# Grouped-query attention on one core: a new instruction plan, v's casts tied to VectorE passes, and reordered first loads

## The chip, the cores and the metric

The kernel runs on one core of a Trainium2 chip. A core has several engines with an instruction queue each: TensorE (matrix products, PE in the profile, with its weight loads shown apart as PEld), VectorE (DVE), ScalarE (ACT), GpSimd (POOL) and SyncE (SP, which here only issues transfers). The metric is the device time of one execution in microseconds. The profile's span, from the first to the last instruction of the program, is somewhat shorter than that time.

## The reference, cut to what matters

```python
# q: (8 batches, 8 heads, 1024, 64); k, v: (8 batches, 2 heads, 1024, 64), float32
for g in range(2):                                  # four q heads share one k and one v
    scores = (1 / 8) * matmul(q[:, 4*g:4*g+4], k[:, g:g+1].transpose(0, 1, 3, 2))
    attn = exp(scores - max(scores))
    attn = attn / (sum(attn) + 1e-8)
    output[:, 4*g:4*g+4] = matmul(attn, v[:, g:g+1])
```

There are 64 jobs (one for each batch and q head). A job has 1024 x 1024 scores. The kernel cuts them into 8 "pairs", each a tile of 128 partitions x 1024 scores in PSUM, the accumulators of TensorE. There are thus 512 pairs, and each must get its exponential. The scores are small, and no maximum is subtracted.

## The kernel before

The exponentials are shared between two engines. Most pairs go to ScalarE, which does one activation for each. The others go to VectorE, which builds the exponential from bits: one pass over the scores in PSUM (`dpass`, tile `yt`), and then, for two pairs at a time, three steps on 16-bit tiles in SBUF: `zh` and `two` (bit masks) and `mul`. For the last two jobs a fourth step, `add`, joins the two parts; for the others TensorE multiplies both parts (`et`, `zt`) with v and so adds them in its accumulator.

```python
# one event of the plan after the other; the engines' queues get their instructions in this order
elif kind == "score":                               # TensorE: one pair, two matmuls
    where_s[(j, c)] = new_slot(x)                   # one of three PSUM slots
    ...
elif kind == "act":                                 # ScalarE: one pair
    exps.append(nc.scalar.activation(out=p, in_=where_s[(j, c)], func=AF.Exp, scale=scale))
    if len(exps) % 12 == 0 and len(exps) > 16: ...  # waits for an exp 15 back
elif kind == "dpass":                               # VectorE: one pair
    nc.vector.tensor_scalar(out=yt[ch][:, i, :, :], in0=where_s[c],
                            scalar1=EXP_A, scalar2=EXP_B, op0=ALU.mult, op1=ALU.add)
elif kind == "zh": ...                              # zt = (yt & 0x7F) | 0x3F00
elif kind == "two": ...                             # et = yt & 0x7F80
elif kind == "mul": ...                             # zt = yt * zt
elif kind == "pv": ...                              # TensorE: products with v into ops (65 columns: 64 and the sum)
elif kind == "rec": ...                             # VectorE: reciprocal of 7 sums
elif kind == "norm": ...                            # VectorE: seven 64-column results times their reciprocals
```

The order of the queues comes from a `Plan` that runs on the host while the kernel is built. It steps through time with a duration for each instruction (`M_ACT` for an exp, `M_FIX + 1024 * M_D1` for a dpass, and so on) and takes at each moment the first choice that its rules allow. Up to two of a job's eight pairs go to VectorE.

v reaches SBUF as float32, and GpSimd casts it into the matmul operand `va`, one tile for each batch and v head, sixteen in all. The plan puts the cast at a fixed time before its first use:

```python
def place_v(b, g):
    return nc.gpsimd.tensor_copy(out=va[:, b * G + g, :, :, 0:D], in_=vs.pop((b, g))...)
...
ev.append((pvs[j] - 16000, "lv", None, (b, g), None))            # load of v
ev.append((max(pvs[j] - 8000, M_START), "pl", None, (b, g), None))   # the cast
```

The start of the kernel loads k, q and v of the first job, casts k and q and turns them with the identity matrix on TensorE:

```python
nc.sync.dma_start(out=f32["k"], in_=rows(k[0, 0], True))
nc.scalar.dma_start(out=f32["q"], in_=rows(q[0, 0], True))
load_v(0, 0)
...
nc.vector.tensor_copy(out=b16["k"], in_=f32["k"])
nc.scalar.activation(out=b16["q"], in_=f32["q"], func=AF.Copy)
# 4 + 4 transposes of k and q, 8 of k with its halves swapped
nc.vector.tensor_copy(out=k0[:, 0, 0:128], in_=turned["k"][:, 0:128])
nc.scalar.activation(out=qt[0][:, 0, :], in_=turned["q"], func=AF.Copy)
nc.vector.tensor_copy(out=k0[:, 0, 128:HS], in_=turned["k"][:, 128:HS])
nc.vector.tensor_copy(out=k0[:, 1, :], in_=ops[0])
```

At the end the last job's result is normalised in two halves on VectorE, each with its own reciprocal, and stored by two transfers.

Of the kernel before, what the change touches and what calls it, by code (L numbers as in the profile page):

```python
# [10 lines left out]
M_START = 5450  # L11
M_SWAP = 1200
M_Q1 = 3500
M_QSTEP = 2700
M_WARM = 7000
M_FILL = 12000
# [4 lines left out]
M_SWITCH = 92  # L21
M_MM = 33.5
M_PVTAIL = 180
M_ACT = 905
M_ATAIL = 135
M_FIX = 76
M_DTAIL = 83
# [4 lines left out]
M_REC = 115  # L32
M_GAP = 60
M_RUNWAY = 1500
M_BACK = 2500
M_WAIT = 200
STEP = 10
INF = float("inf")
PB = 7
NPIECE = 8  # L40
GRAIN = 3
MXD = 2
TAIL = 2
STEPS = (("zh", M_D4), ("two", M_D4), ("mul", M_D2), ("add", M_D2))


class Plan:


    def __init__(self, nj, npt, nct, nyt):  # L50
        self.nj, self.npt, self.nct, self.nyt = nj, npt, nct, nyt
        self.ev = []
        self.spare = None
        self.mms = [8] * nj

        self.last = (nj - 1) * NPIECE
        self.groups = [(i, min(i + PB, self.last)) for i in range(0, self.last, PB)]
        self.groups += [(self.last, self.last + 4), (self.last + 4, self.last + 8)]
        self.group_of = [g for g, (lo, hi) in enumerate(self.groups) for _ in range(lo, hi)]
        self.run()  # L60

    def run(self):
        nj, ev = self.nj, self.ev
        todo = [list(range(8)) for _ in range(nj)]
        dcount = [0] * nj
        qready = [M_START] + [M_START + M_Q1 + M_QSTEP * j for j in range(nj - 1)]
        slot_free = [M_START, M_START, M_START + M_SWAP - 600]
        aq, dq = [], []
        p_ready = [[INF] * 8 for _ in range(nj)]
        tP = tA = M_START  # L70
        tD = M_START + M_SWAP
        mode = None
        steps = list(range(8))
        dend, dlast = 0, None
        open_chain, chains, nch = None, [], 0
        norms = []
        out_free = [M_START, M_START]
        pc, done = 0, 0
        last, groups, group_of = self.last, self.groups, self.group_of
        used_p = used_c = 0  # L80
        a_of = [0] * nj
        ch_left = {}
        a = 0

        def steps_of(j):
            return STEPS if j >= nj - TAIL else STEPS[:3]

        def pick_d():
            for j in range(a, min(nj, a + 3)):
                if todo[j] and dcount[j] < MXD and qready[j] <= tP:  # L90
                    return j
            return None

        while pc < last or steps or norms:
            t = min(tP, tA, tD)
            while a < nj and not todo[a]:
                a += 1
            if tA == t:
                if aq and aq[0][0] <= t:
                    _, s, j, c = aq.pop(0)  # L100
                    ev.append((t, "act", s, j, c))
                    tA = t + M_ACT
                    slot_free[s] = p_ready[j][c] = tA + M_ATAIL + M_SEE
                else:
                    tA = t + STEP
                continue
            if tD == t:
                end = None
                if dq and dq[0][0] <= t:
                    _, s, j, c = dq.pop(0)  # L110
                    if open_chain and open_chain["steps"] != steps_of(j):
                        chains.append(open_chain)
                        open_chain = None
                    if open_chain is None:
                        open_chain = dict(id=nch, pairs=[], at=0, steps=steps_of(j))
                        ch_left[nch] = set()
                        nch += 1
                        used_c += 1
                    ch = open_chain
                    ch["pairs"].append((j, c))  # L120
                    ch_left[ch["id"]].add(j)
                    ev.append((t, "dpass", s, (ch["id"], len(ch["pairs"]) - 1), (j, c)))
                    end = t + M_FIX + 1024 * M_D1
                    slot_free[s] = end + M_DTAIL + M_SEE
                    dlast = (ch["id"], 0)
                    if len(ch["pairs"]) == 2:
                        chains.append(ch)
                        open_chain = None
                elif norms and norms[0][0] <= t and norms[0][1] == "rec":
                    _, _, lo, hi = norms[0]  # L130
                    ev.append((t, "rec", (lo, hi), None, None))
                    end = t + M_REC
                    dlast = lo
                    norms[0] = (end, "norm", lo, hi)
                else:
                    best = None
                    if norms and norms[0][0] <= t:
                        late = dlast == norms[0][2]
                        best = (late, 5 if late else 0, None)
                    for ch in chains:  # L140

                        late = dlast == (ch["id"], ch["at"]) and ch["at"] in (0, 3)
                        key = (late, 3 - ch["at"], ch)
                        if best is None or key[:2] < best[:2]:
                            best = key
                    if best:
                        at = max(t, dend + M_DEP) if best[0] else t
                        ch = best[2]
                        if ch is None:
                            _, _, lo, hi = norms.pop(0)  # L150
                            ev.append((t, "norm", (lo, hi), None, None))
                            end = at + M_FIX + 64 * (hi - lo) * M_D1
                            out_free[group_of[lo] % 2] = end + M_DTAIL + M_SEE
                            dlast = None
                        else:
                            n = len(ch["pairs"])
                            kind, rate = ch["steps"][ch["at"]]
                            ev.append((t, kind, None, ch["id"], n))
                            end = at + M_FIX + 1024 * n * rate
                            ch["at"] += 1  # L160
                            dlast = (ch["id"], ch["at"])
                            if ch["at"] == len(ch["steps"]):
                                chains.remove(ch)
                                for j, c in ch["pairs"]:
                                    p_ready[j][c] = end + M_DTAIL + M_SEE
                if end:
                    tD, dend = end, end + M_DTAIL
                else:
                    tD = t + STEP
                continue  # L170

            cold = 2 if t < M_WARM else 1
            free = [s for s in range(3) if slot_free[s] <= t]
            runway = tA - t + M_ACT * len(aq)
            slack = runway - cold * M_PAIR - M_PTAIL - (M_SWITCH if mode != "s" else 0)
            can_a = a < nj and len(aq) < 2 and qready[a] <= t and used_p < self.npt
            dj = None
            if not dq and len(chains) < self.nyt and (open_chain or used_c < self.nct):
                back = max(tD - t, 0)
                for ch in chains:  # L180
                    n = len(ch["pairs"])
                    back += sum(M_FIX + 1024 * n * r for _, r in ch["steps"][ch["at"] :])
                if back < M_BACK:
                    dj = pick_d()
            kind = None
            if free:
                if dj is not None:
                    if not can_a:
                        kind = "D"
                    elif len(free) > 1 or slack <= M_GAP or mode == "s":  # L190
                        kind = "D" if slack > M_PAIR else "A"
                elif can_a:
                    full = len(free) > 1 or mode == "s"
                    if slack <= M_GAP or (full and runway < M_RUNWAY):
                        kind = "A"
            if kind:
                if mode != "s":
                    tP += M_SWITCH
                    mode = "s"
                s = free[0]  # L200
                j = a if kind == "A" else dj
                c = todo[j].pop(0)
                ev.append((tP, "score", s, j, c))
# [6 lines left out]
                else:  # L210
                    dcount[j] += 1
                    if j < nj - TAIL:
                        self.mms[j] += 1
# [463 lines left out]
```

The softmax here doesn't subtract the row's maximum and nothing guards it: scores larger than these inputs give would overflow.

## Time and profile before

| what | value |
|---|---|
| device time, median of 3 runs | 366.85 us (366.73 to 367.86) |
| span of the profiled execution | 364.9 us |
| ScalarE busy | 355.1 us, 97% of the span |
| VectorE busy | 351.6 us, 96% |
| TensorE busy, matmuls | 346.3 us, 95% |
| GpSimd busy | 51.3 us, 14% |
| transfers | 44.81 MB, mean 123 GB/s |

Busy time of an engine is the time in which at least one of its instructions is under way. Neighbouring instructions of one engine overlap a little, so the mean duration of a group is longer than the distance from one start to the next. For TensorE's matmuls the overlap is large, and its busy share says little. In a row of the groups, "x384" is the count, then come the busy time of the group and the mean duration of one, and after the bar the idle time before them and what ended it.

### The profile page before, as it was taken

The page shows a single profiled execution, that of the slowest core. Times are in us where ns is not written, and L with a number is a line of the kernel's source. Part 1 is how long each engine was busy: PE and PEld are TensorE (multiplying, and loading weights), DVE is VectorE, ACT ScalarE, POOL GpSimd, SP SyncE. Part 2 cuts the span into 40 slices and gives each one's busy share as a digit, 9 for nine tenths or more (in the row PEclk, how much of TensorE's full clock was granted, in tenths as well). Part 3 has the DMA queues.
Part 4 walks back from the last instruction along what each step waited for, and adds up shares of the span by engine and source line. Part 5 has one row for each costly group of instructions (what it writes and reads, how often), then busy time and mean ns, then how long its engine had stood idle before and what let it go on. Part 6 is the DMA issues. An engine that isn't in the chain of part 4 may idle for free.

```text
span 364.9 us, 13795 instructions
## 1 busy us (share of the span) xinstructions
PE 346.3 (95%) x6155; PEld 220.5 (60%) x6155; DVE 351.6 (96%) x476; ACT 355.1 (97%) x387; POOL 51.3 (14%) x100
## 2 busy tenths in 40 slices
PE   7899999999999999999999999999999999999995
PEld 3466666656666665666656666655666656666664
DVE  3999999999999999999999999999999999999993
ACT  4999999999999999999999999999999999999994
POOL 3112021021211112021111112102111111211000
PEclk9999999999999999999999999999999999999999
DMA  6546768659657566856558576567685648953223
GB/s 158 94 97 120 128 121 130 156 107 159 119 89 160 120 146 99 164 111 138 132 102 156 108 141 137 125 150 107 110 164 108 145 79 157 145 122 91 69 59 88
DMA packets 89164, 44.81 MB, mean 123 GB/s; under 512 B 45488, under 2 KB 87345, under 8 KB 87857
## 3 DMA queue, kind: packets, MB, share of 16 engines
q1 hardware_dynamic: 86192, 33.31, 39.6%
q0 software_dynamic: 2496, 10.23, 21.3%
q8 instruction: 48, 0.79, 0.9%
q10 hardware_dynamic: 416, 0.39, 0.4%
q14 instruction: 12, 0.09, 0.1%
HBM read 25.17 MB, written 27.00 MB: 143 GB/s over the span
## 4 chain that ended last, share of the span: by engine, by line
ACT 56%; DVE 37%; PE 4%; DMA 1%; issue 1%
ACT pt L532 56%; DVE yt L543 16%; DVE zt L566 8%; DVE zt L550 5%; DVE ost L633 4%; DVE et L557 4%; PE sp L522 2%; DMA k<-in_k_dram 1%; DVE rec L630 1%; PE ops L584 1%; PE sp L605 1%; PE sp L438 0%; PE ops L428 0%; ACT qt L451 0%; DVE k L433 0%
## 5 line engine op out<-in xcount | busy, mean ns | idle before, releaser
L532 ACT ACTIVATE pt<-sp 128x1024 bf16<-128x1024 f32 x384 | 352.6, 1099 | 1.0 <-PE sp L522 0.7
L522 PE MATMUL sp<-qt,kt 64*128 64x512 bf16 x1024 | 173.4, 385 | 12.2 <-ACT pt L532 6.6
L584 PE MATMUL ops<-va,pt 128*128 128x65 bf16 x3024 | 184.6, 194 | 0.0
L584 PEld LDWEIGHTS <-pt 128*128 128x128 bf16 x3024 | 135.9, 97 | 43.2 <-issue 43.2
L543 DVE TENSOR_SCALAR yt<-sp 128x1024 uint16<-128x1024 f32 x128 | 155.8, 1217 | 2.3 <-PE sp L522 2.1
L584 PE MATMUL ops<-va,zt 128*128 128x65 bf16 x1008 | 124.5, 194 | 0.0
L584 PE MATMUL ops<-va,et 128*128 128x65 bf16 x992 | 120.3, 194 | 0.0
L584 PEld LDWEIGHTS <-et 128*128 128x128 bf16 x992 | 80.3, 98 | 26.0 <-issue 26.0
L584 PEld LDWEIGHTS <-zt 128*128 128x128 bf16 x1008 | 83.2, 97 | 6.9 <-issue 6.9
L522 PEld LDWEIGHTS <-kt 64*128 64x128 bf16 x1024 | 47.5, 93 | 57.6 <-issue 36.7
L566 DVE TENSOR_TENSOR zt<-yt,zt 128x2048 bf16<-128x2048 bf16 x64 | 78.0, 1220 | 0.0
L359 POOL DMA_DIRECT2D qd<-in_q_dram x63 | 32.7, 519 | 214.6 <-PE sp L522 208.5
L550 DVE TENSOR_SCALAR zt<-yt 128x2048 uint16<-128x2048 uint16 x64 | 46.4, 724 | 0.1
L633 DVE TENSOR_TENSOR ost<-ops,rec 128x448 f32<-128x448 f32 x72 | 44.2, 614 | 0.0
L557 DVE TENSOR_SCALAR et<-yt 128x2048 uint16<-128x2048 uint16 x64 | 43.2, 676 | 0.0
L367 POOL DMA_DIRECT2D kd<-in_k_dram x15 | 7.3, 488 | 64.5 <-PE sp L522 59.7
L630 DVE RECIPROCAL rec<-ops 128x7 f32<-128x7 f32 x72 | 14.1, 196 | 1.4 <-PE ops L584 1.3
L384 POOL CAST va<-vs 128x512 bf16<-128x512 f32 x16 | 10.9, 679 | 0.1
L428 PE MATMUL ops<-warm 128*128 128x128 bf16 (+1 forms) x27 | 4.8, 332 | 1.2 <-DVE warm L351 1.2
L428 PEld LDWEIGHTS <-warm 128*128 128x128 bf16 x27 | 2.2, 117 | 4.0 <-issue 2.9
L433 DVE CAST k<-k 128x512 bf16<-128x512 f32 x1 | 0.4, 427 | 2.8 <-DMA k<-in_k_dram 2.8
L434 ACT ACTIVATE q<-q 128x512 bf16<-128x512 f32 x1 | 0.6, 631 | 1.9 <-DMA q<-in_q_dram 1.9
(26 smaller groups left out, 16.4 us busy)
## 6 DMA issues: line engine op xcount, KB each, us to landing
out_dram<-ost SPq DMA_DIRECT2D x63, 256.0 KB, 2.9
qd<-in_q_dram POOLq DMA_DIRECT2D x63, 128.0 KB, 3.3
vs<-in_v_dram SPq DMA_DIRECT2D x16, 256.0 KB, 3.6
kd<-in_k_dram POOLq DMA_DIRECT2D x15, 128.0 KB, 2.9
kt<-kt SPq DMA_DIRECT2D x30, 64.0 KB, 2.8
qt<-qd SPq DMA_TRANSPOSE x63, 3.9
q<-in_q_dram ACTq DMA_DIRECT2D x1, 256.0 KB, 3.6
k<-in_k_dram SPq DMA_DIRECT2D x1, 256.0 KB, 3.7
```

The lines of the kernel that those rows point to most:

```text
L359: return nc.gpsimd.dma_start(out=t.rearrange("(a x) d -> a (x d)", x=4), in_=q[b, h].rearrange("(a x) d -> a (x d)", x=8),)
L367: return nc.gpsimd.dma_start(out=t.rearrange("(a x) d -> a (x d)", x=4), in_=k[b, g].rearrange("(a x) d -> a (x d)", x=8),)
L384: return nc.gpsimd.tensor_copy(out=va[:, b * G + g, :, :, 0:D], in_=vs.pop((b, g)).rearrange("p c (two d) -> p c two d", two=2),)
L522: now = nc.tensor.matmul(sps[x][:, half, :], lhsT=t[lo : lo + D, c // NH, ci % NH * 128 : (ci % NH + 1) * 128], rhs=qt[j][lo : lo + D, 0, ...
L532: exps.append(nc.scalar.activation(out=p, in_=where_s[(j, c)], func=AF.Exp, scale=scale))
L543: nc.vector.tensor_scalar(out=yt[ch][:, i, :, :], in0=where_s[c], scalar1=EXP_A, scalar2=EXP_B, op0=ALU.mult, op1=ALU.add,)
L550: nc.vector.tensor_scalar(out=zt[j][:, 0:c], in0=yt[j][:, 0:c], scalar1=0x7F, scalar2=0x3F00, op0=ALU.bitwise_and, op1=ALU.bitwise_or,)
L557: ins = nc.vector.tensor_scalar(out=et[j][:, 0:c], in0=yt[j][:, 0:c], scalar1=0x7F80, scalar2=None, op0=ALU.bitwise_and,)
L566: nc.vector.tensor_tensor(out=z, in0=yt[j].bitcast(BF16)[:, 0:c], in1=z, op=ALU.mult)
L584: nc.tensor.matmul(ops[plan.group_of[x] % 2][:, lo : lo + D + 1], lhsT=p[:, qs * 128 : (qs + 1) * 128], rhs=va[:, b * G + h // HPG, ci % N ...
L630: nc.vector.reciprocal(out=rec[:, 0:n], in_=o[:, :, D])
L633: nc.vector.tensor_tensor(out=ost[:, r : r + n, :], in0=o[:, :, 0:D], in1=rec[:, 0:n].unsqueeze(2).to_broadcast([128, n, D]), op=ALU.mult,)
```

## The change

The change has four parts.

1. **The plan.** Its durations are set anew: an exp from 905 to 917 ns, the fixed part of a VectorE instruction from 76 to 66 ns, a product with v from 33.5 to 31.2 ns, and others. Where TensorE has several things that it could do, the plan now tries each on a copy of its state, runs on for 7 us and adds up the idle time of ScalarE (weight 1.0) and of VectorE (weight 0.4); the choice with the least is taken. Buffers grow to fit (`pt` from 32 to 34, the chain's tiles from 7 to 8 and from 3 to 4), while k's and v's shrink (from 5 to 4, from 3 to 2). Jobs 1 and 33 may give VectorE three pairs.
2. **The casts of v.** A cast now becomes an event (`gplace`) just ahead of a VectorE pass over PSUM, and waits for the VectorE instruction in front of that pass, so that it begins when the pass begins.
3. **The first loads.** k comes in two pieces, the first v load waits until half of q is cast, the casts and the copies of k and q are shared out between VectorE and ScalarE, and the eight swapped transposes of k come behind the first score.
4. **The end.** The last job has one reciprocal over 8 sums; VectorE normalises one half and ScalarE the other with four small activations.

There is also code for doing part of `mul` on GpSimd; the constant `GC = 0` leaves it out of the program.

Counted in the order of instructions of the two kernels: exps on ScalarE go from 384 to 382, `dpass` from 128 to 130, `zh`, `two` and `mul` from 64 to 65 each, products with v from 5088 to 5104.

```diff
-M_ACT = 905
+M_ACT = 917
-M_FIX = 76
+M_FIX = 66
-M_MM = 33.5
+M_MM = 31.2
+HORIZON = 7000
+W_A = 1.0
+W_D = 0.4
+MORE = 32
+GC = 0
...
+            if s.nxt[j] < 8 and s.dcount[j] < MXD + (j % MORE == 1) and self.qready[j] <= s.tP:
...
+            kind, others = self.choices(s)
+            if others and HORIZON:
+                best = self.cost(s.copy(), kind, t + HORIZON)
+                for x in others:
+                    c = self.cost(s.copy(), x, t + HORIZON)
+                    if c < best - 1:
+                        best, kind = c, x
...
-    NPT = 32
-    NCT = 7
-    NYT = 3
+    NPT = 34
+    NCT = 8
+    NYT = 4
...
-    nc.sync.dma_start(out=f32["k"], in_=rows(k[0, 0], True))
+    for c, n in ((0, 1), (1, NH - 1)):
+        nc.sync.dma_start(out=f32["k"][:, c : c + n], in_=rows(k[0, 0], True)[:, c : c + n])
     nc.scalar.dma_start(out=f32["q"], in_=rows(q[0, 0], True))
-    load_v(0, 0)
...
-    nc.vector.tensor_copy(out=b16["k"], in_=f32["k"])
-    nc.scalar.activation(out=b16["q"], in_=f32["q"], func=AF.Copy)
+    nc.vector.tensor_copy(out=b16["k"][:, 0:1], in_=f32["k"][:, 0:1])
+    ins = nc.scalar.activation(out=b16["q"][:, 0:2], in_=f32["q"][:, 0:2], func=AF.Copy)
+    nc.vector.tensor_copy(out=b16["q"][:, 2:NH], in_=f32["q"][:, 2:NH])
+    nc.scalar.activation(out=b16["k"][:, 1:NH], in_=f32["k"][:, 1:NH], func=AF.Copy)
+    tc.add_manual_dep(load_v(0, 0).ins, ins.ins.name, Sync, reason="loads in time, not sooner")
...
+        elif kind in ("gmul", "gplace"):
+            if kind == "gplace":
+                gps = place_v(*divmod(j, G))
...
+            tc.add_manual_dep(gps.ins, vec.ins.name, Sync, reason="VectorE needs the port before")
...
-            if len(exps) % 12 == 0 and len(exps) > 16:
+            if len(exps) % (NPT - 6) == 0:
...
+                if lo >= plan.last:
+                    for i in range(4):
+                        nc.scalar.activation(
+                            out=ost[:, r + 4 + i, :], in_=o2[:, 1, i, 0:D],
+                            func=AF.Copy, scale=rec[:, 4 + i : 5 + i],
+                        )
```

## The prediction, made before the result was known

> **What bounds the kernel now.** I read the groups of the page first. Columns: line, engine, operation, tiles and shapes, count; after the first bar busy time in us and mean ns of one; after the second the idle time before them and what ended it.
>
> ```profile
> L532 ACT ACTIVATE pt<-sp 128x1024 bf16<-128x1024 f32 x384 | 352.6, 1099 | 1.0 <-PE sp L522 0.7
> L522 PE MATMUL sp<-qt,kt 64*128 64x512 bf16 x1024 | 173.4, 385 | 12.2 <-ACT pt L532 6.6
> L543 DVE TENSOR_SCALAR yt<-sp 128x1024 uint16<-128x1024 f32 x128 | 155.8, 1217 | 2.3 <-PE sp L522 2.1
> L566 DVE TENSOR_TENSOR zt<-yt,zt 128x2048 bf16<-128x2048 bf16 x64 | 78.0, 1220 | 0.0
> L550 DVE TENSOR_SCALAR zt<-yt 128x2048 uint16<-128x2048 uint16 x64 | 46.4, 724 | 0.1
> ```
>
> The exps keep ScalarE busy for 352.6 of 364.9 us with 1.0 us of idle time among them, and VectorE is also hardly ever idle. TensorE's scores wait 12.2 us, 6.6 of them for ScalarE to give a PSUM slot back: TensorE is ahead. So two engines are full at once, and the page alone does not say which one has room. The chain that ended last, taken piece by piece (start, length, what), tells more.
>
> ```profile
> 0.74 3.75 DMA k<-in_k_dram
> 9.41 19.00 ACT pt L532 x21
> 138.44 11.22 ACT pt L532 x12
> 349.28 9.18 ACT pt L532 x10
> ```
>
> 21 exps in 19.00 us are 0.905 us each; the piece at 138.44 shows 0.935. All in all ScalarE starts its first exp at 7.36 and ends its last at about 360.28, so 352.9 / 384 = 0.919 each. Compared with 0.905 that is 384 x 0.014 = 5.4 us that an exp waited for a score that came late, in waits too short to be shown as idle time. For VectorE I read the timeline of single instructions (start, length) at two casts of v, and GpSimd's beside it.
>
> ```profile
> 182.13 1.82 DVE L566 TENSOR_TENSOR zt<-yt,zt 128x2048 bf16<-128x2048 bf16 x1
> 183.87 0.19 DVE L630 RECIPROCAL rec<-ops 128x7 f32<-128x7 f32 x1
> ...
> 203.68 1.22 DVE L543 TENSOR_SCALAR yt<-sp 128x1024 uint16<-128x1024 f32 x1
> 204.81 0.61 DVE L633 TENSOR_TENSOR ost<-ops,rec 128x448 f32<-128x448 f32 x1
> 205.34 0.68 DVE L550 TENSOR_SCALAR zt<-yt 128x2048 uint16<-128x2048 uint16 x1
> 205.94 1.22 DVE L543 TENSOR_SCALAR yt<-sp 128x1024 uint16<-128x1024 f32 x1
> ```
>
> ```profile
> 182.23 0.63 POOL L384 CAST va<-vs 128x512 bf16<-128x512 f32 x1
> ...
> 204.26 0.63 POOL L384 CAST va<-vs 128x512 bf16<-128x512 f32 x1
> ```
>
> Distances between starts are the real cost: 1.13 us for a dpass, 0.53 for a norm, 0.60 for a mask step; read so along the timeline, the others are 1.13 for a mul, 0.61 for `zh` and 0.12 for a reciprocal. The mul at 182.13 stands beside a cast and takes 183.87 - 182.13 = 1.74, so 0.61 us are lost. The cast at 204.26 stands beside a dpass and a norm, and nothing is lost. I went through all sixteen: nine met a mask step or a mul and cost 0.24 to 0.80 us, 4.4 us together.
>
> **What the Trainium skill says.** "SBUF — State Buffer", section "Who interferes with whom": VectorE shares a port pair with GpSimd; an instruction in a two-port mode, and one with two SBUF inputs against a GpSimd reader, takes it for its whole length and the other blocks, while a VectorE instruction with at most one SBUF input outside those modes does not contend. The two casts above agree: the PSUM pass and the norm (one SBUF input) are untouched, the mul is held. "VectorE: DVE Perf Modes", section "The perf-mode tier table", gives 693 ns for a 16-bit `tensor_scalar` of 2048 and 1224 ns for a `tensor_tensor`; the trace has 0.68 and 1.22 us where nothing is beside them. "ScalarE: Activation LUTs", section "What ACT_TABLE_LOAD costs", puts an activation at 186 ns + 0.833 ns per column, 93 ns more for each pointer operand, and an overlap of about 93 ns back to back: 946 ns for an exp by that, where the trace shows 905, so the measurement is used.
>
> **The change part by part.**
>
> *Work moved to VectorE.* Two exps leave ScalarE: 2 x 0.905 = 1.8 us less. VectorE gets 2 x 1.13 + 0.61 + 0.60 + 1.13 = 4.6 us more. TensorE gets 16 products of 0.031 us (ten stand in 0.47 us of the timeline, less the length of one), 0.5 us, for which it has room.
>
> *Casts.* The sixteen casts stay, fifteen of them begin with a PSUM pass (1.13 us), and a cast takes 0.63. If GpSimd's queue is free at that moment, the 4.4 us go. So on VectorE the casts pay for the two added pairs nearly exactly: +4.6 - 4.4 = +0.2 us.
>
> *First loads.* Before, k lands at 4.49, then cast, eight transposes, copy of q (ends 6.68), score, exp at 7.36. After, q needs a half-width cast (0.4), four transposes (0.5), a copy of 320 columns (0.45) and the score, with k's other pieces beside it; without v's 256 KB in the way q may land 0.2 us sooner. I estimate the first exp at 6.5, 0.9 sooner. But VectorE's first dpass (7.79 before) stands in its queue behind the copy of the swapped k, which now waits for transposes that follow the first score: 6.4 + 0.65 + 0.7 = 7.8, no gain.
>
> *Plan.* What the look-ahead is worth cannot be counted from the source. The order of instructions shows that TensorE's pattern hardly changes: 272 runs of scores between products, 270 before. At best it removes ScalarE's 5.4 us of late scores.
>
> *End.* Before, two normalisations in a row end 1.18 us after the last sums (360.80 to 361.98). After, four small activations with a pointer operand: by the skill's figures 186 + 93 + 53 - 93 = about 240 ns each, an estimate, 1.0 us, after a 0.2 us reciprocal. No gain, at most 0.2.
>
> ```profile
> 358.49 0.21 DVE L630 RECIPROCAL rec<-ops 128x7 f32<-128x7 f32 x1 [1.33 <-PE ops L584]
> 360.80 0.18 DVE L630 RECIPROCAL rec<-sp 128x4 f32<-128x4 f32 x1 [1.45 <-PE sp L605]
> 361.56 0.42 DVE L633 TENSOR_TENSOR ost<-sp,rec 128x256 f32<-128x256 f32 x1
> ```
>
> **The sum, for each engine.** ScalarE: 6.5 + 382 x 0.919 (late scores as before) = 357.6, or 6.5 + 382 x 0.905 = 352.2 with none. From its last exp to the end of the span it was 364.9 - 360.3 = 4.6 us. Span 356.8 to 362.2. VectorE: up to the last dpass there stood 127 dpasses, 64 muls and adds, 63 each of the mask steps, 69 reciprocals and 69 norms: 336.9 us by the distances above. It began at 7.79 and reached the last dpass at 351.14, so 6.4 us were lost: 4.4 to casts, 0.9 between the first two dpasses, 1.1 elsewhere. After: 129, 65, 64, 64, 70, 69 make 341.6. 7.8 + 341.6 + 0.9 + 1.1 = 351.4, later than before by 0.3. Behind it stand 6.9 us of work and waits for the last products; in the lines above these are 1.33 + 1.45 = 2.8 us because ScalarE ended last. With ScalarE ahead I take half, 1.5. VectorE ends at 359.8, and the last store ends the span 2.9 us after it, as before (361.98 to 364.9): 362.7. Device time lay 366.85 - 364.9 = 2.0 above the span: 364.7. The look-ahead also counts VectorE's idle time, and I give it 0.4 us of the 1.1. **So VectorE becomes the bound, and I predict 364.3 us**, 0.7% less than before.
>
> **Rivals.**
> 1. *ScalarE stays the bound with its late scores.* For it: the number of runs of scores is the same, and three PSUM slots still feed both engines. It makes 362.2 + 2.0 = 364.2, nearly the same time, but VectorE would then wait at the end.
> 2. *The look-ahead works fully and VectorE gives way.* ScalarE's 356.8 would make 358.8. Against it: VectorE's 341.6 us to the last dpass are counted work, and no order of scores shortens them. Only a shorter start and end could, so 361 is about the floor.
> 3. *Casts still collide.* GpSimd's queue keeps its order, and q's and k's conversions (0.49 us each, waiting for scores) stand in it. If a cast starts 0.5 us late, it runs into the next mask step. With all 4.4 us back: 368 to 369.
> 4. *The plan fits less well.* It now takes 917 ns for an exp that needs 905, so it may issue scores later than ScalarE wants them. Another 3 to 5 us of late scores: 367 to 369.
>
> **Range and chances.** 364.3 is where the first two sums meet. The low end, 361.0, is rival 2 at its floor; the high end, 367.8, a half of rival 3 or 4. Over 2% faster means below 359.5, which VectorE's counted work all but excludes: 0.03. Over 2% slower means above 374.2, more than rivals 3 and 4 bring together: 0.04. That leaves 0.93 within 2%.
>
> **What would show it right or wrong.** In the profile after: casts that begin just behind the start of a dpass, and no mul or mask step above 1.3 us (step *casts*); first exp at 6.3 to 6.7 and first dpass at 7.6 to 8.0 (*first loads*); ScalarE's exps at 0.919 or longer on average with VectorE never waiting (VectorE the bound), or at 0.905 to 0.91 with VectorE's last dpass before 350 (I undercounted what the look-ahead gains); the chain's share of VectorE well above the 37% of before. A plan that leaves TensorE waiting less, and the exps longer apart, would make the prediction too low; a dpass that starts well before 7.6, or work of VectorE that I count as fixed but that shrinks, would make it too high.

## The result, and the profile after

The changed kernel takes 364.33 us at the median, the kernel before 367.37 us in the same session: a ratio of 0.9923, 95% interval 0.990 to 0.9946. It is faster by 0.8%, about 2.8 us. The predicted time was 364.3 us. Three of the six executions of the kernel before in that session took 367.86 to 368.00 us; in the four later sessions, with 113 executions, its medians are 366.63 to 366.87 us, and against those the gain is 2.3 to 2.5 us.

The chain that ended last (share of the span by engine), before the change and then after it:

```profile
ACT 56%; DVE 37%; PE 4%; DMA 1%; issue 1%
```

```profile
ACT 94%; PE 4%; issue 1%; DVE 0%
```

The groups that answer to those of before, in the same columns:

```profile
L747 ACT ACTIVATE pt<-sp 128x1024 bf16<-128x1024 f32 x382 | 350.7, 1067 | 2.0 <-PE sp L735 2.0
L735 PE MATMUL sp<-qt,kt 64*128 64x512 bf16 x1024 | 174.2, 383 | 8.9 <-ACT pt L747 4.9
L758 DVE TENSOR_SCALAR yt<-sp 128x1024 uint16<-128x1024 f32 x130 | 158.4, 1218 | 1.3 <-PE sp L735 1.1
L781 DVE TENSOR_TENSOR zt<-yt,zt 128x2048 bf16<-128x2048 bf16 x65 | 78.4, 1207 | 0.0
L765 DVE TENSOR_SCALAR zt<-yt 128x2048 uint16<-128x2048 uint16 x65 | 44.1, 679 | 0.2
```

Two things are to be seen. The chain lies on ScalarE for 94% of the span, where 37% were VectorE's before. And the mask step `zh` has come down from 724 to 679 ns on average, the mul from 1220 to 1207: nothing holds them any more. The timeline at a cast, GpSimd's first and then VectorE's, shows why:

```profile
128.93 0.62 POOL L552 CAST va<-vs 128x512 bf16<-128x512 f32 x1 [1.55 <-DVE et L772]
```

```profile
128.93 1.23 DVE L758 TENSOR_SCALAR yt<-sp 128x1024 uint16<-128x1024 f32 x1
130.07 0.61 DVE L855 TENSOR_TENSOR ost<-ops,rec 128x448 f32<-128x448 f32 x1
130.60 1.22 DVE L781 TENSOR_TENSOR zt<-yt,zt 128x2048 bf16<-128x2048 bf16 x1
```

The cast starts with the dpass, is done after 0.62 us and leaves it its 1.14 us (128.93 to 130.07). All sixteen casts lie within a dpass (the first begins 0.37 us behind its start, the others within 0.18 us of it), and none stands beside a mask step or a mul. VectorE has room at the end: its last reciprocal waits 2.42 us for TensorE's last products, which wait for ScalarE's last exps.

```profile
358.70 0.21 DVE L852 RECIPROCAL rec<-sp 128x8 f32<-128x8 f32 x1 [2.42 <-PE sp L820]
```

The profiled execution took 365.4 us, 1.1 more than the median, because TensorE's granted clock fell to a half for 3.4 us in it; that stretch is set apart below. The two profiles add up as follows, all from starts and ends in the timelines (0.903 and 0.904 us are the commonest distances of two exps):

| part of the span, us | before | after |
|---|---|---|
| up to the first exp | 7.36 | 6.33 |
| 383 or 381 distances of exps at 0.904 | 346.23 | 344.42 |
| what the distances are longer than that (late scores) | 5.47 | 6.28, of which 1.48 at the low clock |
| the last exp | 1.21 | 1.15 |
| from its end to the issue of the last store | 1.74 | 2.23 |
| from there to the end of the span | 2.85 | 3.21 |
| span | 364.87 | 363.62 |

So in these two profiles the start gives 1.0 us and the two exps 1.8; late scores fall by 0.7 outside the low clock, 0.25 of it in the first 12 us; the end takes back 0.5 and more. The 1.0 us of the start is a figure of two single executions: in the eleven traces of kernels with the new start the first exp begins between 6.12 and 6.78 us, most often near 6.56.

### The profile page after: what moved, and what is told of

It reads as the page before. It is cut to its first block, busy times and chain, and to the rows that moved or that the text cites. A ratio compares the mean times of both kernels' runs of the same rounds, so it can differ in the third digit from the quotient of the medians.

```text
span 363.6 us, 13853 instructions
## 1 busy us (share of the span) xinstructions
PE 348.0 (96%) x6179; PEld 222.5 (61%) x6179; DVE 350.6 (96%) x481; ACT 354.3 (97%) x390; POOL 50.2 (14%) x100
## 4 chain that ended last, share of the span: by engine, by line
ACT 94%; PE 4%; issue 1%; DVE 0%
ACT pt L747 94%; PE ops L799 1%; PE ops L600 1%; PE sp L735 1%; PE sp L820 1%; ACT ost L863 0%; ACT qt L624 0%; DVE qt L626 0%; DVE warm L519 0%; PE sp L614 0%
## 5 line engine op out<-in xcount | busy, mean ns | idle before, releaser
L747 ACT ACTIVATE pt<-sp 128x1024 bf16<-128x1024 f32 x382 | 350.7, 1067 | 2.0 <-PE sp L735 2.0
L799 PE MATMUL ops<-va,pt 128*128 128x65 bf16 x3008 | 182.7, 194 | 0.0
L799 PEld LDWEIGHTS <-pt 128*128 128x128 bf16 x3008 | 140.4, 98 | 34.2 <-issue 34.2
L758 DVE TENSOR_SCALAR yt<-sp 128x1024 uint16<-128x1024 f32 x130 | 158.4, 1218 | 1.3 <-PE sp L735 1.1
L799 PE MATMUL ops<-va,zt 128*128 128x65 bf16 x1024 | 136.9, 195 | 0.0
L799 PE MATMUL ops<-va,et 128*128 128x65 bf16 x1008 | 133.9, 195 | 0.0
L799 PEld LDWEIGHTS <-et 128*128 128x128 bf16 x1008 | 86.1, 98 | 30.6 <-issue 30.0
L799 PEld LDWEIGHTS <-zt 128*128 128x128 bf16 x1024 | 88.8, 98 | 7.6 <-issue 7.6
L781 DVE TENSOR_TENSOR zt<-yt,zt 128x2048 bf16<-128x2048 bf16 x65 | 78.4, 1207 | 0.0
L765 DVE TENSOR_SCALAR zt<-yt 128x2048 uint16<-128x2048 uint16 x65 | 44.1, 679 | 0.2
L820 PE MATMUL sp<-va,pt 128*128 128x65 bf16 x48 | 1.9, 194 | 0.5 <-ACT pt L747 0.5
```

Source lines behind the costliest of these rows:

```text
L758: vec = nc.vector.tensor_scalar(out=yt[ch][:, i, :, :], in0=where_s[c], scalar1=EXP_A, scalar2=EXP_B, op0=ALU.mult, op1=ALU.add,)
L765: vec = nc.vector.tensor_scalar(out=zt[j][:, 0:c], in0=yt[j][:, 0:c], scalar1=0x7F, scalar2=0x3F00, op0=ALU.bitwise_and, op1=ALU.bitwise_or,)
L781: vec = nc.vector.tensor_tensor(out=z, in0=flat(yt[j])[:, 0:c, 0 : cols[0]], in1=z, op=ALU.mult)
L799: nc.tensor.matmul(ops[plan.group_of[x] % 2][:, lo : lo + D + 1], lhsT=p[:, qs * 128 : (qs + 1) * 128], rhs=va[:, b * G + h // HPG, ci % N ...
```

## The experiments

Two theories stood against each other. *VectorE*: its counted work sets the end. *ScalarE*: the exps, their late scores and the way to the first and from the last one set it, and VectorE has room. "Over the changed kernel" below is the difference of the medians; the four later medians of the kernel before lie within 0.24 us of each other. All ratios are to the kernel before.

In a part of the executions TensorE's granted clock falls to a half for 3.4 us or more, which shows as a mean clock under 0.996. In the changed kernel these took 365.4 us and the others 364.2. Some kernels had many of them and others none, so the medians are given without them too:

| kernel | executions | median, us | with a fall of the clock | median of the others, us (lowest to highest) |
|---|---|---|---|---|
| before, four later sessions | 113 | 366.63 to 366.87 | 18 | 366.54 to 366.79 by session |
| changed | 6 | 364.33 | 2 | 364.19 (363.76 to 364.41) |
| casts at fixed times | 22 | 367.72 | 18 | 366.60 (366.50 to 366.66) |
| two pairs back | 22 | 365.93 | 0 | 365.93 (365.43 to 366.33) |
| tie alone, kernel before | 14 | 366.70 | 5 | 366.54 (365.56 to 366.73) |
| VectorE relieved | 18 | 365.04 | 10 | 364.28 (364.24 to 364.71) |
| look-ahead off | 10 | 365.09 | 6 | 364.51 (364.50 to 364.51) |
| first loads as before | 22 | 366.86 | 11 | 366.14 (364.72 to 366.52) |
| end as before | 6 | 363.80 | 2 | 363.78 (363.71 to 363.82) |
| own tile for the activations | 6 | 364.93 | 4 | 364.18 (364.09 and 364.26) |
| activations ahead | 7 | 364.99 | 4 | 364.34 (364.24 to 364.43) |
| third pair in jobs 5 and 37 | 6 | 363.91 | 0 | 363.91 (363.66 to 364.55) |
| the same, activations ahead | 5 | 363.99 | 0 | 363.99 (363.63 to 364.22) |
| the same, end as before | 4 | 363.52 | 0 | 363.52 (363.06 to 363.73) |

### The casts at fixed times again

```diff
-    ev = list(plan.ev)
+    ev = [e for e in plan.ev if e[1] != "gplace"]
+    ev.append((max(pvs[j] - 8000, M_START + 100), "pl", None, (b, g), None))   # no tie
```

The edit also puts v's loads back to a fixed time, as in the kernel before.

> The changed kernel, with v's sixteen casts put back to a fixed time before their first use and tied to no VectorE instruction; every other queue keeps its order. VectorE (the engine of the prediction): the 4.4 us of held steps come back and VectorE sets the end, so 364.3 + 4.4 = 368 to 369. ScalarE (rival): VectorE waited 2.4 us for the last products in the changed kernel and has that much room, so at most 4.4 - 2.4 = 2 us come back, 364.3 to 366.3. Both expect mask steps and muls above 1.3 us beside casts again.

Measured: 367.72 us, ratio 1.0024 (1.0012 to 1.0035), 3.4 us over the changed kernel, and 2.4 us without a fall of the clock. The VectorE timeline, of an execution without one, shows a mul held beside GpSimd's cast (289.77 to 291.73 = 1.96 us, where 1.13 is usual):

```profile
289.77 2.03 DVE L781 TENSOR_TENSOR zt<-yt,zt 128x2048 bf16<-128x2048 bf16 x1
291.73 1.21 DVE L758 TENSOR_SCALAR yt<-sp 128x1024 uint16<-128x1024 f32 x1
```

```profile
290.10 0.62 POOL L552 CAST va<-vs 128x512 bf16<-128x512 f32 x1
```

Five steps are held for 0.57 to 0.83 us each, 3.4 us together. The median alone would speak for VectorE's theory (4.4 us back); without a fall of the clock the 2.4 us are close to what the ScalarE theory allowed (2 us). The waits (who waited for whom: us, times, longest), one line of the changed kernel and then three of this one, say how the loss gets to the end:

```profile
PE sp L735 <- DVE yt L758: 0.6, 2, 0.3
```

```profile
PE sp L735 <- DVE yt L758: 2.5, 7, 0.6
...
DVE rec L852 <- PE sp L820: 2.4, 1, 2.4
...
ACT pt L747 <- PE sp L735: 2.3, 5, 0.9
```

In the changed kernel TensorE waits for VectorE's slots twice, 0.6 us; here seven times, 2.5 us. A dpass that is late keeps its PSUM slot, TensorE's queue stops at the next score, and ScalarE runs short: its distances lose 7.7 us to late scores, where those of the changed kernel lose 4.8 outside its stretch of low clock. VectorE still has its 2.4 us of idle time before the last reciprocal, so the time was lost by way of ScalarE, and not at VectorE's end.

### Two pairs back to ScalarE

```diff
-s.dcount[j] < MXD + (j % MORE == 1)
+s.dcount[j] < MXD
```

> The changed kernel without the third pair of jobs 1 and 33: 128 pairs on VectorE and 384 on ScalarE, as before the change; the plan is made anew with that. VectorE bounds: 4.6 us of its work go, and the time falls to 360 to 362.5. ScalarE bounds: two exps of 0.905 us more, the time rises by 1.8 to about 366. The order of instructions shows fifteen exps in a row after VectorE's last pair, in place of nine; if that costs ScalarE's late scores nothing, it is neutral for both.

Measured: 365.93 us, ratio 0.9978 (0.9969 to 0.9987), 1.6 us over the changed kernel, and 1.7 without a fall of the clock. That is the 1.8 us of two exps: ScalarE bounds. VectorE, with 4.6 us less to do, began its last dpass at 344.83 us and not at 349.63, and the kernel still took longer.

### The tie alone, in the kernel before

```diff
+            if late_v:
+                gps = place_v(*late_v.pop(0))
+                tc.add_manual_dep(gps.ins, vec.ins.name, Sync, reason="with a VectorE pass")
             vec = nc.vector.tensor_scalar(out=yt[ch][:, i, :, :], ...)
```

> The kernel before, with one thing changed: each cast of v waits for the next VectorE pass over PSUM and begins with it. ScalarE bounds the kernel before: VectorE gains its 4.4 us and only waits longer at the end, 367.4 less at most 0.8. VectorE's held steps also keep PSUM slots and so make scores late: 2 to 4 us less, 363.5 to 365.5, with the mean distance of exps below 0.919.

Measured: 366.7 us, ratio 0.9999 (0.9984 to 1.0014): nothing. Fifteen of the sixteen casts hold no step any more; one still holds a mask step by 0.3 us. A part of VectorE's gained time shows up as waits for scores:

```profile
DVE yt L550 <- PE sp L526: 3.6, 8, 1.1
```

It was 2.1 us in four waits before; the longest one here, 1.1 us, lies behind a fall of the clock that the profiled execution had. So the 4.4 us of held steps cost the old plan nothing, and cost the new plan 2.4 us and more. That this is so because the new plan fills VectorE is argued and not shown: no run has the new plan untied and without the two moved pairs.

### VectorE relieved of 39 us

```diff
-                    yield ci, et[ch].bitcast(BF16)[:, i, par, :]
+                    yield ci, zt[ch].bitcast(BF16)[:, i, par, :]
...
-            vec = ins = nc.vector.tensor_scalar(out=et[j][:, 0:c], ...)   # 65 mask steps left out
+            ins = vec
```

> The changed kernel without VectorE's `two` step: the 65 mask steps that make et are left out, TensorE multiplies zt in the place of et, so the products are as many but the values are not those of the reference. VectorE has 65 x 0.60 = 39 us less, the order of the other instructions is unchanged. VectorE bounds, or its fullness makes the scores late: exps come down to 0.905 us each, first exp 6.3 + 345.7 + 5 + 2 = 359. Late scores come from TensorE's order and the three slots alone: 364, unchanged within 0.7.

Measured: 365.04 us, ratio 0.9958 (0.9944 to 0.9972), 0.7 us over the changed kernel and not below it. Its groups:

```profile
L747 ACT ACTIVATE pt<-sp 128x1024 bf16<-128x1024 f32 x382 | 350.9, 1067 | 2.8 <-PE sp L735 2.8
L758 DVE TENSOR_SCALAR yt<-sp 128x1024 uint16<-128x1024 f32 x130 | 158.8, 1222 | 25.7 <-PE sp L735 24.6
```

VectorE now waits 24.6 us for scores ahead of its passes, and ScalarE is busy for 350.9 us, against 350.7. From 31 us on, behind the low clock of both profiles, late scores cost ScalarE 4.7 us here and 4.6 in the changed kernel. This decides between the theories: VectorE's work does not set the end, and the late scores do not come from its being full. The 0.7 us lie in the clock: ten of the 18 executions had a fall (6.8 us long in the profiled one), and the others are at 364.28 us, as the changed kernel's.

### The look-ahead off

```diff
-HORIZON = 7000
+HORIZON = 0
```

> The changed kernel with the look-ahead off (HORIZON = 0): the plan takes its first choice at each moment, as before the change, with the new durations and all other parts of the change. If the look-ahead brings the gain by fewer late scores: exps go from 0.917 on average (outside the stretch of lower clock) to 0.92 or more, and the time rises by 1 to 3 us. If the gain comes from the two exps moved, the start and the tied casts: within 0.7 us of the changed kernel.

Measured: 365.09 us, ratio 0.9955 (0.994 to 0.9969), 0.8 us over the changed kernel, and 0.3 without a fall of the clock; the intervals overlap. The profile has 5.7 us of late scores, 0.65 of them in one exp at the low clock, so some 5.0 against the changed kernel's 4.8. The look-ahead is worth some 0.3 us, a microsecond at most.

### The first loads as before

```diff
-    dummy(8, HS)                  # warm-up matmuls
+    dummy(6, HS)
-    # k in two pieces, v's load held back, casts shared out, swapped transposes behind the first score
+    # k whole, v at once, k cast on VectorE and q on ScalarE, all transposes ahead
```

> The changed kernel with the first loads and casts of the kernel before (k whole, v at once, swapped transposes ahead of the first score); the plan is the same. ScalarE bounds: the first exp goes back from 6.33 to about 7.36 and the end moves by the same 1.0 us. VectorE bounds: its first pass goes from 7.29 to 7.8, 0.5 us. If the start is taken up by later waits: nothing.

Measured: 366.86 us, ratio 0.9997 (0.9982 to 1.0012), 2.5 us over the changed kernel. The first exp is at 6.81 in the profile, only 0.5 later than in the changed kernel's and 0.25 later than in most kernels with the new start. The edit takes back one more thing that came with the change: eight warm-up matmuls (their results are not used) on TensorE at the start, where the kernel before has six. The chains of the kernel before and of this one at the same eight transposes show TensorE's pace:

```profile
4.99 1.05 PE sp L438 x8
```

```profile
5.08 0.64 PE sp L609 x8
```

The first six score matmuls took 1.46 us before and 0.82 here. So TensorE ran more slowly at the start of the profile of before. The page shows a clock of 1.00 there, but the trace's record of the clock begins only at 10.35 us, where it begins at 4.54 here and between 4.18 and 6.87 in the eleven traces with eight warm-up matmuls. So part of the 1.0 us between the profiles before and after was TensorE's pace and not the loads. What the loads do themselves is seen in ScalarE's cast of q, which waits for q's transfer: it begins at 3.72 us in the changed kernel and at 4.36 here.

Why the median rose by 2.5 us is open in part. Eleven of the 22 executions had a fall of the clock (367.2 to 368.0 us). Four took 364.7 to 365.0 us, only 0.5 to 0.8 over the changed kernel; the profiled one, of 364.88 us, is of these. The other seven took 365.9 to 366.5 us, and no trace shows why. A TensorE that stays slow longer at the start, as in the trace of before, would fit; no run separates the two warm-up matmuls from the loads.

### The end as before

```diff
-    vec = nc.vector.reciprocal(out=to, in_=sums)          # 8 sums at once
-    nc.scalar.activation(...)                             # x4
+    # reciprocal of 4, normalise, reciprocal of 4, normalise, all on VectorE
```

> The changed kernel with the end of the kernel before: two reciprocals and two normalisations in a row on VectorE, no small activations on ScalarE. In the profiles the last store is issued 1.74 us after the last exp before, and 2.23 us after it in the changed kernel, so the old end should be 0.5 us faster. If the prediction's working is right (no gain, at most 0.2), the same within 0.2.

Measured: 363.80 us, ratio 0.9924 (0.9907 to 0.9942): 0.5 us less than the changed kernel, and 0.4 without a fall of the clock. The intervals overlap, but the mechanism is plain in the timelines, the changed kernel's ScalarE first, then this one's:

```profile
359.45 0.93 ACT L863 ACTIVATE ost<-sp,rec 128x64 f32<-128x64 f32 x4 [1.27 <-PE sp L820]
360.41 0.41 ACTq L831 DMA_DIRECT2D out_dram<-ost  x1
```

```profile
349.58 7.47 ACT L747 ACTIVATE pt<-sp 128x1024 bf16<-128x1024 f32 x8
358.79 0.40 ACTq L831 DMA_DIRECT2D out_dram<-ost  x1
```

The last exp ends at 358.18 there and at 357.05 here, so the last store follows it by 2.23 and 1.74 us. The new end is 0.5 us slower up to the store.

### A tile of their own for the small activations, and their place ahead

```diff
-out=ost[:, r + 4 + i, :], in_=o2[:, 1, i, 0:D],
+out=ost2[:, i, :], in_=o2[:, 1, i, 0:D],
```

> The changed kernel with the four small activations at the end writing to a tile of their own, not to the ring of results. Their first one then needs no semaphores of old stores, only VectorE's and TensorE's. In the changed kernel it begins 0.54 us after the reciprocal has ended. If the waits for old stores cost that: it begins 0.1 us after, and the time falls by 0.4 to 0.5 us. If it is held by something else, as the normalisation on VectorE: no change.

Measured: 364.93 us, ratio 0.9942 (0.9923 to 0.9962), no gain (364.18 us without a fall of the clock, the changed kernel 364.19); the store still follows the last exp by 2.23 us. The old stores were not the cause. The other order, the four activations given out ahead of the normalisation:

> The changed kernel with the four small activations of the end given out ahead of the last normalisation on VectorE; nothing else. With a tile of their own they still began 0.09 us after that normalisation had ended. If they wait for it only because it stands ahead of them: they now begin less than 0.1 us after the reciprocal and the last store is issued 0.45 us sooner. If something else holds them: no change.

Measured: 364.99 us, ratio 0.9947 (0.9927 to 0.9968). ScalarE and VectorE at the end of this kernel:

```profile
357.94 0.93 ACT L857 ACTIVATE ost<-sp,rec 128x64 f32<-128x64 f32 x4 [0.76 <-DVE rec L852]
358.90 0.40 ACTq L831 DMA_DIRECT2D out_dram<-ost  x1
```

```profile
357.70 0.21 DVE L852 RECIPROCAL rec<-sp 128x8 f32<-128x8 f32 x1 [2.43 <-PE sp L820]
358.90 0.42 DVE L861 TENSOR_TENSOR ost<-sp,rec 128x256 f32<-128x256 f32 x1 [1.00 <-ACT ost L857]
```

The activations now begin 0.03 us after the reciprocal (357.91), but VectorE waits for them, and its store is the late one, 2.17 us after the last exp. So whichever of the two engines comes second waits for the first. Both read the same PSUM tile. The Trainium skill, "PSUM — Partial Sum Buffer", section "PSUM bank collisions raise a hardware error", says that two engines must not be on one bank at once and that an order is put between them; here the two halves lie in two banks of one tile, and the order is there all the same. That the shared tile is the reason is argued: a tile of their own for the results changed nothing, and no run gave the halves PSUM tiles of their own. In this form the two engines' shares of the step do not overlap.

### The third pair in other jobs

In the changed kernel's order TensorE has ten pairs of scores in a row at the second job, with no products between them, for the job waits for its third VectorE pair. (The very first pairs, 14 in a row, also have no products, but warm-up matmuls between them.)

```diff
-s.dcount[j] < MXD + (j % MORE == 1)
+s.dcount[j] < MXD + (j % MORE == 5)
```

> The changed kernel with the third VectorE pair in jobs 5 and 37, not 1 and 33; the number of pairs on each engine stays 130 and 382. In the changed kernel's order TensorE has ten pairs of scores in a row, with no products between, at the second job (waiting for its third VectorE pair), and its profile shows the clock at a half for 3.4 us right behind; here the longest run is six. If that idle stretch brings the clock down: no dip in most runs (mean clock 0.996 and above), ScalarE loses 1 to 1.5 us less, 363 to 364 where the changed kernel has 364 to 365.4. If the clock dips on its own: as the changed kernel, dips in half of the runs.

Measured: 363.91 us, ratio 0.9915 (0.9897 to 0.9933). Two stretches of both kernels (us from the start; length; busy us and count of TensorE, its weight loads, VectorE, ScalarE, GpSimd; granted clock; share and rate of transfers), the changed kernel first:

```profile
21.00:25.00 4.00, 2.26 (x14) 0.69 (x13) 4.00 (x5) 4.00 (x6) 1.02 (x2) 1.00 0.18 42
25.00:29.00 4.00, 4.00 (x52) 2.68 (x50) 3.17 (x5) 2.85 (x4) 0.39 (x1) 0.57 0.26 37
```

```profile
21.00:25.00 4.00, 3.94 (x83) 2.70 (x80) 4.00 (x6) 4.00 (x6) 0.60 (x1) 1.00 0.27 37
25.00:29.00 4.00, 4.00 (x76) 2.44 (x72) 4.00 (x7) 4.00 (x5) 0.69 (x2) 1.00 0.38 58
```

The changed kernel has 14 matmuls from 21 to 25 us, then a clock of 0.57 for four microseconds, and ScalarE is busy for only 2.85 of the 4.00. With the third pair moved TensorE has 83 matmuls there, the clock stays at 1.00 and ScalarE loses nothing. The chain of the changed kernel shows the low clock in its products, 25 of them in 1.49 us (0.060 each, where ten stand in 0.47 us with the length of one at full clock):

```profile
25.21 1.49 PE ops L799 x25
```

Counted over all executions: of the seven kernels with the changed kernel's order of scores and products, 51 of 87 executions had a mean clock under 0.996; of the four without a run of more than six pairs behind the start (this one, the two below and the one with two pairs back) none of 37. The kernel with the look-ahead off has the run of ten too, and a fall in six of ten executions. So the run is what brings the clock down in these kernels, but not every time: with the end as before the profiled execution has the same run, 12 matmuls from 21 to 25 us, and the clock stays at 1.00.

What moving the pair saves is mostly the falls: without one the changed kernel takes 364.19 us and this kernel 363.91, and the late scores of the two outside the low clock are the same, 4.8 us.

Together with the activations put ahead:

> The third pair in jobs 5 and 37, and the four small activations ahead of the last normalisation. If both gains are real and add up: 1.0 us at the median from the first and 0.45 from the second, 0.988 of the kernel before (362.5 to 363). If the clock is not tied to the run of scores: 0.991.

Measured: 363.99 us, ratio 0.9915 (0.9899 to 0.9932): the clock's part came, the end's did not, as above. The best version takes the third pair in jobs 5 and 37 and the end of the kernel before:

> The third pair in jobs 5 and 37 and the end of the kernel before (two reciprocals and two normalisations on VectorE). The first keeps the clock up, the second issues the last store 1.74 us after the last exp in place of 2.23. If they add up: 363.9 - 0.5 = 363.4, 0.990 of the kernel before, last store issued 1.7 to 1.8 us after the last exp, no dip of the clock. If the closing of the program (0.9 to 1.4 us after the last landing) takes it up: 363.9.

Measured: 363.52 us, ratio 0.991 (0.9894 to 0.9927), last store 1.74 us after the last exp (357.07 to 358.81), the clock at 1.000. It is the fastest of all at the median and surely faster than the kernel before; against the changed kernel the intervals overlap, and the ratios say 0.5 us, the medians 0.8.

## Why the prediction was right or wrong

The time was right by luck: the reason given for it was not.

- *VectorE becomes the bound.* Wrong; this is the step that failed. VectorE has room at the end, and even 39 us less work on it did not shorten the kernel. In the sum, the part up to VectorE's last dpass was 351.4 predicted and 349.63 measured: the start of 7.8 was 7.29 (the swapped transposes took 0.41 us, not 0.65), the wait of 0.9 behind the first dpass was 0.33, and of the 1.1 us "elsewhere" some 0.4 were left. VectorE then waited 2.4 us for the last products, not 1.5. Of the signs named for this bound the distance of exps came, but VectorE did wait, and its share of the chain is 0% and not well above 37%.
- *Rival 1, ScalarE stays the bound with its late scores.* This is what happened. It gave 364.2: exps at 0.919 on average (measured 0.921, or 0.917 without the low clock), first exp at 6.5 (measured 6.33), and 4.6 us behind the last exp, which is the mis-sized term: 5.4.
- *Casts.* Right: all sixteen lie within a pass and nothing is held. What the step missed is that the 4.4 us were worth nothing to the kernel before (ratio 0.9999 with the tie alone).
- *Work moved to VectorE.* Right in size: two pairs back cost 1.6 to 1.7 us where 1.8 was counted.
- *End.* Wrong by its order, not its sizes: the four activations take 0.93 us, 1.0 was estimated from the Trainium skill's figures. But they do not run beside the normalisation, so 0.5 us were lost where no change was predicted.
- *Plan.* The 0.4 us allowed were VectorE's, of its 1.1 us lost elsewhere; 0.7 went. That the plan would also make the run of ten pairs of scores, behind which the clock falls, was not foreseen.

VectorE's sum also has a slip. In the kernel before the last dpass begins at 351.14, and the 6.9 us counted behind it begin with the reciprocal:

```profile
351.14 1.22 DVE L543 TENSOR_SCALAR yt<-sp 128x1024 uint16<-128x1024 f32 x1
352.28 0.20 DVE L630 RECIPROCAL rec<-ops 128x7 f32<-128x7 f32 x1
```

So the 1.13 us of the last dpass itself stand in no term. With them VectorE's sum is 365.8 and not 364.7. The term left out (1.1) and the part that came out too long (351.4 for 349.63) pull against each other, which is how the wrong sum stayed near the measured time. And the time alone could not have told 364.2 from 364.7.

## What to carry to other kernels

When two engines are full to the last per cent, relieve one of them on the chip before saying which sets the end; the counted sums were too close to tell. A stall on an engine off the path can be free in one plan and cost in another: 4.4 us of held steps cost the old plan nothing, 3.4 us of them cost the new one 2.4 us. Look in the order of instructions for stretches in which TensorE has little to do: from 21 to 25 us ScalarE lost nothing by it, but the clock fell behind. And when a disturbance strikes some executions and not others, compare kernels without it too; the medians alone put the casts at 3.4 us and VectorE's relief at a loss.

## What the runs showed of the hardware

TensorE's clock fell to a half in the changed kernel's profile though no idle gap of TensorE from 20 to 25 us was longer than 0.53 us; it ran fourteen matmuls in the last 4 us ahead of the fall. The fall lasted 3.41 us, or 6.83 in the kernel with VectorE relieved. In all five traces with such a fall only 10 to 12 matmuls, scores alone, start in the 3.41 us directly ahead of it. One of the five is the kernel before with the tie, where the fall (16.15 to 19.56 us) comes behind its first scores, so the run of ten pairs at the second job is not the only stretch that does it. The Trainium skill, "TensorE: Matmul & The Clock Gate", section "Part 1: The HAM clock gate (the "warmup" mystery)", gives about 3.4 us for the window in which activity is watched, and the lengths agree. That little work, and not idleness alone, can bring the clock down is what moving the third pair shows here: 51 of 87 executions had a fall with the run of ten pairs, none of the 15 with the third pair moved. Why the other 36 had none is not shown. One such fall cost ScalarE 1.5 us in the changed kernel's profile.
